# Eight experts of the first block: float32 weights, four experts on quarters of the columns

## The chip, the core and the metric

One core of one Trainium2 chip runs the whole program. The metric is the device time of one launch in microseconds (us). The kernel before takes 1819.28 us, the median of three runs that lie between 1818.02 and 1819.74. The engines are named as in the profile: PE is the matrix engine (TensorE), PEld its weight loads, DVE the VectorE, ACT the ScalarE, POOL the GpSimd, SP the engine that issues most transfers.

## What is computed

Four layers act on 256 tokens of 1024 features. Layers one and two (attention mixers, then a dense feed-forward and a layer of 8 experts) make the first block; layers three and four (two recurrent mixers, each with a layer of 16 experts) the second. The change is in the expert layer of the first block:

```python
def swiglu(h, w_gu, w_dn):
    gu = h @ w_gu
    g, u = jnp.split(gu, 2, axis=-1)
    return (jax.nn.silu(g) * u) @ w_dn

def moe_swiglu(h, w_router, w_gu_e, w_dn_e):     # 8 experts, w_gu 1024 x 2816, w_dn 1408 x 1024
    logits = (h @ w_router).astype(jnp.float32)
    top_val, top_idx = lax.top_k(logits, TOP_K)  # TOP_K = 2
    top_w = jax.nn.softmax(top_val, axis=-1)
    combine = jnp.sum(jax.nn.one_hot(top_idx, N_EXPERTS, dtype=jnp.float32) * top_w[..., None], axis=-2)
    ...
    for e in range(N_EXPERTS):
        out = out + combine[..., e:e + 1] * swiglu(h, w_gu_e[e], w_dn_e[e])
```

Each token goes to 2 of 8 experts, so an expert gets 64 of the 256 tokens on average; on the reference's inputs the fullest gets 76. All is float32.

## The kernel before

**Slots.** `moe1` works on gathered tokens. `router` and `ranks` give each chosen token a slot number within its expert, and a one-hot matrix `P` of 128 slots per expert gathers the tokens by a product (`gather`). An expert with more tokens than slots is done again by `overflow`, behind a branch on a count (`flag`); on these inputs it isn't entered.

**Split weights.** Everything that is multiplied with weights goes through a split of float32 numbers into a high and a low part of the faster type float32r: `hilo` (L462) lets ACT write the high part and DVE the difference. A product then is three matmuls (`mm3`): high by high, high by low, low by high. Weights arrive in tiles `raw` of 128 x 2048 float32 (a unit, 1 MB), five of them in a ring (`rp`), are split by `split` into tiles `hi` and `lo` (six each, `sp`), and the matmuls read these.

**The loop of the first expert layer.** `experts` runs jobs of (expert, 256 columns of gate and up): 8 chunks of the 1024 features give gate and up side by side in one bank of PSUM (512 columns), `swiglu` makes the hidden values, `turn` transposes them and splits them into `fh` and `fl`, and `down` adds their product with the matching rows of the second weight to two banks per expert. Six jobs to an expert, the last half as wide; the products up and down alternate. When an expert is finished its 128 x 1024 result is split (`y_split`), scattered back to the tokens by a product with the transposed one-hot matrix (`scatter`) and added to `xt` with the router's weight.

**Filling the router's wait.** The choice of experts is a chain of small DVE operations. While it runs, PE computes half of the first expert's first job for all 256 tokens (`dense` in `router`, whose weights are split ahead, partly into tiles `wide`), and only the hidden values are gathered later (`early`).

**The other expert layers** (`moe2`, `pairs`) already keep their weights float32: units go to a ring of 11 places (`RING`; five `raw`, six pairs of `hi` and `lo` tiles), are read by PE as they are, and two experts of 64 slots each stand on the two halves of the array's 128 columns: each matmul has a stationary operand 64 columns wide, and its result lands on half of the partitions. In these layers the router's wait is not filled. The program writes one float32 matmul; the trace shows two records for it.

**Order.** SP issues all weight transfers in the order that `sequence` lists, each as soon as its tile is free. The order on the engines is that of the code, except that a scheduler moves an instruction ahead where another would wait.

Of the kernel before, what the change touches and what calls it, by code (L numbers as in the profile page):

```python
# [9 lines left out]
F32 = mybir.dt.float32  # L10
F32R = mybir.dt.float32r
# [7 lines left out]
T = 256  # L19
# [10 lines left out]
HALF = 64  # L30
RING = 11
# [77 lines left out]

def rows_dn(w):  # L110
    return units(rows_k(w)[None])


def pack(inp):
# [29 lines left out]
    out["m1d"] = np.stack([rows_k(a["w_dn_exp"][0][e]) for e in range(NE1)])  # L144
# [42 lines left out]
class Kern:  # L187
# [123 lines left out]
    def sequence(self):  # L311
# [11 lines left out]
        m1 = []  # L323
        for e in range(NE1):
            for j in range(6):
                g = [(p["m1g"][e, 2 * j + i], UNIT) for i in range(2 if j < 5 else 1)]
                n = min((j + 1) * UNIT, FE * 8)
                m1.append((g, [(p["m1d"][e, :, j * UNIT:n], n - j * UNIT)]))

# [7 lines left out]
        jobs(m1)  # L337
# [24 lines left out]
    def load_plain(self):  # L362
# [12 lines left out]
        for h in range(2):  # L375
            for o in range(0, UNIT // 2, m):
                s = h * UNIT // 2 + o
                self.nc.sync.dma_start(halves[h][:, o:o + m], ap[:, s:s + m])
# [763 lines left out]

    def gather_spare(self, hh, hl):
# [296 lines left out]

    def overflow(self, flag, rk, C, hh, hl, n, F, gu, dn, after=None, cap=CAP):
# [7 lines left out]
        with tc.If(v > cap):  # L1449
# [9 lines left out]
            with tc.For_i(0, n, 1) as e:  # L1459
# [3 lines left out]
                for j in range(nt):  # L1463
# [16 lines left out]
                    nc.sync.dma_start(wt[:, :nch].rearrange("p k n -> p (k n)"), dn(e, j, nch * D))  # L1480
# [21 lines left out]
    def moe1(self):  # L1502
        nc = self.nc
        h = [self.xn[tb] for tb in range(2)]
        ps, hh, hl = self.router("router1", h, NE1)
# [8 lines left out]
        for tb in range(2):  # L1514
            self.dense(tb, range(0 if tb else EARLY, KC))
        first = self.gather(hh, hl, rk, 0)
# [12 lines left out]
        self.tt(C, C, o2, ALU.add)  # L1529
        m1g, m1d = self.p["m1g"], self.p["m1d"]  # L1530

        def add(b, tb, hf, n, ps):
            if b == NE1 - 1 and tb and hf:
                t = self.w2([128, 512], name="part")
                nc.scalar.activation(t, ps, AF.Copy, scale=C[:, tb, b:b + 1])
                nc.gpsimd.tensor_tensor(out=self.xt[:, tb, n], in0=self.xt[:, tb, n], in1=t, op=ALU.add)
            else:
                self.stt(self.xt[:, tb, n], ps, C[:, tb, b:b + 1], self.xt[:, tb, n], ALU.mult, ALU.add)
        jobs = [(e, 256 if j < 5 else 128, j == 0, j == 5, 0) for e in range(NE1) for j in range(6)]
        self.experts(jobs, hh, hl, rk, first, None, add)  # L1540
# [5 lines left out]
        def dn(e, j, n):  # L1546
# [506 lines left out]
```

## Time and profile before

| | us |
|---|---|
| median of three runs | 1819.28 |
| the profiled execution | 1816.75 |
| its span | 1815.0 |
| PE busy in it | 1755.0 (97%) |
| DVE busy, ACT busy | 1073.0, 849.3 |
| first expert layer, from the first gathering matmul to the last scattering one | 411.1 |

The page gives the span in 40 slices of 45.4 us. PE is at nine tenths or more nearly everywhere; the transfers run at 409 GB/s in the two later expert layers and at 320 to 360 GB/s in the first. A matmul's record is longer than the time it occupies the engine, since matmuls are pipelined: what one costs in a stream is the distance of two starts.

### The profile page before, as it was taken

Reading aid. Unit: us, or ns where it says so; the run is one execution under the profiler, and the core shown is the slowest. Engines: PE = TensorE matmul, PEld = TensorE weight load, DVE = VectorE, ACT = ScalarE, POOL = GpSimd, SP = SyncE. Lnnn points to the kernel's source line nnn. Section 1 sums busy time; section 2 is a strip of 40 time slices with the busy share of each in tenths; the row PEclk is TensorE's granted clock in tenths of the full one; section 3 lists DMA queues with packets and bytes.
Section 4 is the critical chain, followed back from the end, with each engine's and each line's share of the span. In section 5 each row is a group of like instructions: output and inputs, shape, how many; then the busy total and the mean of one; then the engine's idle time right before and its main releaser. Section 6 shows DMA issues by size and latency. Waiting matters only on the chain. (4 is left out here: it accounts for less than half of the span.)

```text
span 1815.0 us, 24991 instructions
## 1 busy us (share of the span) xinstructions
PE 1755.0 (97%) x9506; PEld 1279.4 (70%) x9506; DVE 1073.0 (59%) x1616; ACT 849.3 (47%) x1255; POOL 40.3 (2%) x59
## 2 busy tenths in 40 slices
PE   9999999999999999999999899899988998999996
PEld 7977899989878888888887787533424997443332
DVE  6567655455677999998989667321215687222123
ACT  5675544455855777777767542210103654111011
POOL 0000000000000000000000001000000001000000
PEclk9999999999999999999999999899998999999999
DMA  8445555546446599999999745699999556799996
GB/s 333 147 150 180 176 185 185 185 148 200 143 154 226 188 333 325 363 320 335 329 334 332 253 147 181 254 409 409 409 409 343 192 175 220 279 409 409 409 409 240
DMA packets 136436, 491.35 MB, mean 271 GB/s; under 512 B 15329, under 2 KB 15585, under 8 KB 136306
## 3 DMA queue, kind: packets, MB, share of 16 engines
q1 hardware_dynamic: 133794, 480.72, 73.0%
q0 software_dynamic: 2512, 8.91, 1.5%
q8 instruction: 79, 1.29, 0.3%
q14 instruction: 51, 0.42, 0.1%
HBM read 488.52 MB, written 1.05 MB: 270 GB/s over the span
## 5 line engine op out<-in xcount | busy, mean ns | idle before, releaser
L305 DVE TENSOR_TENSOR lo<-raw,hi 128x1024 fp32r<-128x1024 f32 x513 | 616.5, 1220 | 211.6 <-ACT hi L463 200.0
L463 ACT CAST hi<-raw 128x1024 fp32r<-128x1024 f32 x513 | 530.4, 1049 | 247.3 <-PE mm L274 167.1
L274 PE MATMUL mm<-hi,Th 128*128 128x512 f32 (+1 forms) x940 | 364.4, 388 | 2.2 <-ACT Th L463 1.9
L274 PE MATMUL mm<-lo,Th 128*128 128x512 f32 (+1 forms) x940 | 356.5, 379 | 0.6 <-DVE lo L305 0.5
L274 PE MATMUL mm<-hi,Tl 128*128 128x512 f32 (+1 forms) x940 | 356.4, 379 | 0.3 <-DVE Tl L305 0.3
L274 PE MATMUL mm<-Th,hi 128*128 128x256 f32 x768 | 218.0, 284 | 0.0
L274 PE MATMUL mm<-Th,lo 128*128 128x256 f32 x768 | 217.3, 283 | 0.0
L274 PE MATMUL mm<-Tl,hi 128*128 128x256 f32 x768 | 217.2, 283 | 0.0
L274 PEld LDWEIGHTS mm<-hi,Th 128*128 128x128 f32 x940 | 178.8, 190 | 36.3 <-ACT Th L463 4.1
L274 PEld LDWEIGHTS mm<-hi,Tl 128*128 128x128 f32 x940 | 178.1, 190 | 35.9 <-DVE Tl L305 3.3
L274 PEld LDWEIGHTS mm<-lo,Th 128*128 128x128 f32 x940 | 178.8, 190 | 32.6 <-DVE lo L305 2.3
L308 DVE SCALAR_TENSOR_TENSOR hh<-sl,gt,mm 128x256 f32<-128x256 f32 x33 | 15.9, 480 | 243.3 <-ACT sl L445 243.2
L445 ACT ACTIVATE sl<-mm 128x256 f32<-128x256 f32 (+2 forms) x93 | 36.9, 396 | 248.8 <-PE mm L274 248.3
L274 PEld LDWEIGHTS mm<-Th,hi 128*128 128x128 f32 x768 | 147.2, 192 | 1.5 <-ACT hi L463 0.8
L274 PEld LDWEIGHTS mm<-Tl,hi 128*128 128x128 f32 x768 | 147.2, 192 | 0.5
L274 PE MATMUL mm<-raw,xs 128*64 128x512 f32 x512 | 146.9, 598 | 0.6 <-DMA raw<-in_m 0.6
L274 PEld LDWEIGHTS mm<-Th,lo 128*128 128x128 f32 x768 | 147.2, 192 | 0.1
L274 PE MATMUL mm<-hi,xs 128*64 128x512 f32 x272 | 99.5, 603 | 9.0 <-DMA hi<-in_m 8.9
L274 PE MATMUL acc<-hi,fl 128*128 128x512 f32 x264 | 103.9, 397 | 0.6 <-DVE fl L305 0.6
L274 PE MATMUL acc<-lo,fh 128*128 128x512 f32 x264 | 104.4, 395 | 0.0
L274 PE MATMUL acc<-hi,fh 128*128 128x512 f32 x264 | 103.7, 396 | 0.4 <-ACT fh L463 0.4
L274 PE MATMUL mm<-lo,xs 128*64 128x512 f32 x272 | 94.0, 592 | 0.0
(397 smaller groups left out, 2023.2 us busy)
## 6 DMA issues: line engine op xcount, KB each, us to landing
raw<-in_wd SPq DMA_DIRECT2D x250, 512.0 KB, 4.9
raw<-in_m SPq DMA_DIRECT2D x184, 512.0 KB, 10.2
raw<-in_m1g SPq DMA_DIRECT2D x176, 512.0 KB, 6.0
lo<-in_m SPq DMA_DIRECT2D x104, 512.0 KB, 10.2
hi<-in_m SPq DMA_DIRECT2D x104, 512.0 KB, 10.2
raw<-in_m1d SPq DMA_DIRECT2D x87, 512.0 KB, 6.0
bg<-in_b_gate POOLq DMA_DIRECT2D x8, 256.0 KB, 3.6
bc<-in_ln_g POOLq DMA_DIRECT2D x4, 512.0 KB, 6.8
```

The costliest lines, as they stand in the source:

```text
L274: q = self.nc.tensor.matmul(out, lhsT, rhs, start=start, stop=stop, skip_group_check=True)
L305: return self.nc.vector.tensor_tensor(out=out, in0=in0, in1=in1, op=op)
L308: return self.nc.vector.scalar_tensor_tensor(out, in0, scalar, in1, op0=op0, op1=op1)
L445: q = self.nc.scalar.activation(*a, **k)
L463: a = self.nc.scalar.copy(hi, src)
```

## The change

The first expert layer leaves the split of its weights. Its units go to the ring of 11, PE reads them as float32, and four experts at a time stand on the four quarters (32 columns) of the array. An expert has 96 slots now, in three rounds of 32: for every chunk of weights each of the three rounds runs four matmuls, one to an expert (`products`). All of the products up of four experts come first (six steps over the columns), then the products down in two passes, one for each half of the 1024 output columns, over 11 chunks of hidden values. The second weight is laid out anew for that (`rows_h`). `gather12` gathers the slots of four experts in float32, 8 times four matmuls of 384 columns. The router's weight goes into the hidden values (`gate`), so that `add` only adds. `turn` and `scatter` are put off to the middle of the next step (`put_off`). `router` is called with `plain`: the dense half job is gone, and so is what it needed. `overflow` gets the new limit of 96 and the new layout.

```diff
@@ -28,6 +28,8 @@
 FE2 = 512
 CAP = 128
 HALF = 64
+QUART = 32
+ROUNDS = 3
 RING = 11
 ALPHA = (2 * DEPTH) ** 0.25
 RMS_EPS = 1e-6
@@ -105,6 +107,12 @@
 def half_cols(w, i):
 
     return w.rearrange("p (a n) -> p a n", a=2)[:, :, i * 128:(i + 1) * 128]
+
+
+def rows_h(w):
+
+    K, N = w.shape
+    return w.reshape(K // 128, 128, 2, N // 2).transpose(1, 2, 0, 3).reshape(128, -1)
 
 
 def rows_dn(w):
@@ -141,7 +149,7 @@
     out["wd"] = np.concatenate(dense, 0)
     gu = a["w_gu_exp"][0]
     out["m1g"] = np.stack([tiles_gu(gu[e][:, :FE], gu[e][:, FE:]) for e in range(NE1)])
-    out["m1d"] = np.stack([rows_k(a["w_dn_exp"][0][e]) for e in range(NE1)])
+    out["m1d"] = np.stack([rows_h(a["w_dn_exp"][0][e]) for e in range(NE1)])
     out["m2"] = np.stack([
         np.concatenate([tiles_gu(a["moe_w1_2"][l][e], a["moe_w3_2"][l][e]), rows_dn(a["moe_w2_2"][l][e])], 0)
         for l in range(DEPTH) for e in range(NE2)])
@@ -320,13 +328,6 @@
                 seq.append((wd[u], UNIT))
                 u += 1
         dense(2 * nd["mix"] + nd["ffn"])
-        m1 = []
-        for e in range(NE1):
-            for j in range(6):
-                g = [(p["m1g"][e, 2 * j + i], UNIT) for i in range(2 if j < 5 else 1)]
-                n = min((j + 1) * UNIT, FE * 8)
-                m1.append((g, [(p["m1d"][e, :, j * UNIT:n], n - j * UNIT)]))
-
         def jobs(js):
             for i, (g, d) in enumerate(js):
                 seq.extend(g)
@@ -334,7 +335,17 @@
                     seq.extend(js[i - 1][1])
             seq.extend(js[-1][1])
             seq[-1] += (True,)
-        jobs(m1)
+
+        n, nf = len(seq), FE * 4
+        for e0 in range(0, NE1, 4):
+            es = range(e0, e0 + 4)
+            seq.extend((p["m1g"][e, i], UNIT) for i in range(11) for e in es)
+            for hf in range(2):
+                for o in range(0, nf, UNIT):
+                    w = min(UNIT, nf - o)
+                    seq.extend((p["m1d"][e, :, hf * nf + o:hf * nf + o + w], w) for e in es)
+        seq[-1] += (True,)
+        self.plain.update((n + i, i % RING) for i in range(len(seq) - n))
         for l, nm in enumerate(("gla", "mlstm")):
             dense(nd[nm])
             m2 = lambda e, u: (p["m2"][l * NE2 + e, u], UNIT)
...
@@ -1138,6 +1151,25 @@
                     self.mm(v[:, dd], x[tb][:, c], P[:, tb].rearrange("p i s -> p (i s)"),
                             start=dd == 0 and i == 0, stop=dd == 1 and i == 3)
             (nc.vector.tensor_copy if d % 4 else nc.scalar.copy)(xs[:, d:d + 2], v)
+        return xs, P
+
+    def gather12(self, hh, hl, rk, e0):
+
+        nc = self.nc
+        n = ROUNDS * 128
+        shape = [128, ROUNDS, 4, QUART]
+        P = [self.w2([128, n], F32R, name="P") for _ in range(2)]
+        for tb in range(2):
+            q = self.tt(P[tb].rearrange("p (r x s) -> p r x s", r=ROUNDS, x=4),
+                        self.bf["iota"][:, :ROUNDS * QUART].rearrange("p (r s) -> p r s", r=ROUNDS)[:, :, None, :]
+                        .to_broadcast(shape), rk[:, tb, None, e0:e0 + 4, None].to_broadcast(shape), ALU.is_equal)
+        self.fence = q
+        xs = [self.tp.tile([128, 4, n], F32, name="xs", tag="Th") for _ in range(2)]
+        for d in range(KC):
+            ps = self.bank()[:, :n]
+            for i, (x, tb) in enumerate((x, tb) for x in (hh, hl) for tb in range(2)):
+                self.mm(ps, x[tb][:, d * 128:(d + 1) * 128], P[tb], start=i == 0, stop=i == 3)
+            (nc.vector.tensor_copy if d % 2 else nc.scalar.copy)(xs[d // 4][:, d % 4], ps)
         return xs, P
 
     def gather_spare(self, hh, hl):
@@ -1437,6 +1469,111 @@
         p, yh, yl = down(*last, ahead=True)
         self.scatter(yh, yl, PT[p // 2][:, p % 2], final, pre)
         return res
+
+    def fours(self, hh, hl, rk, first, Cs, add):
+
+
+        nc = self.nc
+        X, PT, gate, f, late = {}, {}, {}, {}, []
+        quarters = [slice(x * QUART, (x + 1) * QUART) for x in range(4)]
+
+        def more(g, P):
+            blocks = []
+            for r0 in range(0, ROUNDS, 2):
+                m = min(2, ROUNDS - r0)
+                v = self.bank()[:, :m * T].rearrange("p (e t) -> p e t", e=m)
+                for r in range(m):
+                    for tb in range(2):
+                        self.mm(v[:, r, tb * 128:(tb + 1) * 128], P[tb][:, (r0 + r) * 128:(r0 + r + 1) * 128],
+                                self.identr, start=r == 0 and tb == 0, stop=r == m - 1 and tb == 1)
+                t = self.w2([128, m, T], F32R, name="PT")
+                nc.scalar.copy(t, v)
+                blocks += [t[:, r] for r in range(m)]
+            PT[g] = blocks
+            pg = self.bank("acc")[:, :8 * ROUNDS]
+            for r in range(ROUNDS):
+                for tb in range(2):
+                    self.mm(pg[:, 8 * r:8 * r + 8], P[tb][:, r * 128:(r + 1) * 128], Cs[:, tb, g],
+                            start=r == 0 and tb == 0, stop=r == ROUNDS - 1 and tb == 1)
+            gt = gate[g] = self.wp.tile([128, 4], F32, name="gt", tag="gt", bufs=4)
+            v = pg.rearrange("p (r i n) -> p r n i", r=ROUNDS, i=2)
+            for x, s in enumerate(quarters):
+                nc.vector.tensor_reduce(gt[s, :ROUNDS], v[s, :, x], AX.X, ALU.add)
+
+        def gather(g):
+            X[g], P = self.gather12(hh, hl, rk, 4 * g) if g else first
+            if g:
+                more(g, P)
+
+        def products(out, w, lhs, k, rhs, start, stop):
+            for r in range(ROUNDS):
+                for x, s in enumerate(quarters):
+                    c = r * 128 + x * QUART
+                    self.mm(out[r][s, :w], lhs[:, c:c + QUART], rhs[x](k)[:, :w], start=start, stop=stop)
+
+        def turn(g, j, w, h, tag):
+            if j == 0:
+                t = [self.tp.tile([128, 5, ROUNDS * 128], F32, name="f", tag="Tl") for _ in range(2)]
+                for c in range(10):
+                    f[c] = t[c // 5][:, c % 5]
+            for kk in range(w // 128):
+                c = 2 * j + kk
+                if c == 10:
+                    f[c] = self.w2([128, ROUNDS * 128], name="f10")
+                ps = self.bank(tag)[:, :ROUNDS * 128]
+                for r in range(ROUNDS):
+                    nc.tensor.transpose(ps[:, r * 128:(r + 1) * 128], h[r][:, kk * 128:(kk + 1) * 128], self.ident)
+                (nc.vector.tensor_copy if kk else nc.scalar.copy)(f[c], ps)
+
+        def scatter(g, hf, ys, tag):
+            n = slice(hf * 512, (hf + 1) * 512)
+            for tb in range(2):
+                ps = self.bank(tag)
+                s = slice(tb * 128, (tb + 1) * 128)
+                for r in range(ROUNDS):
+                    self.mm(ps, PT[g][r][:, s], ys[r][:, 0], start=r == 0)
+                    self.mm(ps, PT[g][r][:, s], ys[r][:, 1], stop=r == ROUNDS - 1)
+                add(tb, n, ps)
+
+        def put_off():
+            while late:
+                late.pop(0)()
+
+        gather(0)
+        for g in range(NE1 // 4):
+            for j in range(6):
+                w, kpu = (256, 4) if j < 5 else (128, 8)
+                out = [self.bank("acc" if j % 2 else "mm") for _ in range(ROUNDS)]
+                for k in range(KC):
+                    if k % kpu == 0:
+                        ws = [self.unit(kpu) for _ in range(4)]
+                    if k == 4:
+                        put_off()
+                    products(out, 2 * w, X[g][k // 4][:, k % 4], k % kpu, ws, k == 0, k == 7)
+                if g == 0 and j == 0:
+                    more(0, first[1])
+                h = [self.w1([128, 256], name="hh") for _ in range(ROUNDS)]
+                for r in range(ROUNDS):
+                    self.swiglu(h[r][:, :w], out[r][:, :w], out[r][:, w:2 * w], gate[g][:, r:r + 1])
+                late.append(lambda g=g, j=j, w=w, h=h: turn(g, j, w, h, "acc" if j % 2 else "mm"))
+            for hf in range(2):
+                tag = "acc" if hf else "mm"
+                out = [self.bank(tag) for _ in range(ROUNDS)]
+                for c in range(11):
+                    if c % 4 == 0:
+                        ws = [self.unit(4) for _ in range(4)]
+                        if g and hf and c == 8:
+                            self.split()
+                    if c == 4:
+                        put_off()
+                        if hf and g + 1 < NE1 // 4:
+                            gather(g + 1)
+                    products(out, 512, f[c], c % 4, ws, c == 0, c == 10)
+                ys = [self.a4([128, 2, 512], F32R, name="ys") for _ in range(ROUNDS)]
+                for r in range(ROUNDS):
+                    self.hilo(ys[r][:, 0], ys[r][:, 1], out[r])
+                late.append(lambda g=g, hf=hf, ys=ys, tag=tag: scatter(g, hf, ys, tag))
+        put_off()
...
@@ -1511,9 +1649,7 @@
         S = self.rt(NE1, "S", BF)
         self.tt(S, o1, o2, ALU.add)
         rk, flag = self.ranks(S, NE1, "r")
-        for tb in range(2):
-            self.dense(tb, range(0 if tb else EARLY, KC))
-        first = self.gather(hh, hl, rk, 0)
+        first = self.gather12(hh, hl, rk, 0)
         e = self.rt(1, "gm")
         self.tt(e, m2, m1, ALU.subtract)
         self.act(e, e, AF.Exp)
@@ -1527,25 +1663,24 @@
         self.tt(C, o1, g1.to_broadcast([128, 2, NE1]), ALU.mult)
         self.tt(o2, o2, g2.to_broadcast([128, 2, NE1]), ALU.mult)
         self.tt(C, C, o2, ALU.add)
+        Cs = self.wp.tile([128, 2, 2, 8], F32R, name="Gs", tag="Gs", bufs=1)
+        self.hilo(Cs[:, :, :, :4], Cs[:, :, :, 4:], C.rearrange("p b (g j) -> p b g j", g=2))
         m1g, m1d = self.p["m1g"], self.p["m1d"]
 
-        def add(b, tb, hf, n, ps):
-            if b == NE1 - 1 and tb and hf:
-                t = self.w2([128, 512], name="part")
-                nc.scalar.activation(t, ps, AF.Copy, scale=C[:, tb, b:b + 1])
-                nc.gpsimd.tensor_tensor(out=self.xt[:, tb, n], in0=self.xt[:, tb, n], in1=t, op=ALU.add)
-            else:
-                self.stt(self.xt[:, tb, n], ps, C[:, tb, b:b + 1], self.xt[:, tb, n], ALU.mult, ALU.add)
-        jobs = [(e, 256 if j < 5 else 128, j == 0, j == 5, 0) for e in range(NE1) for j in range(6)]
-        self.experts(jobs, hh, hl, rk, first, None, add)
+        def add(tb, n, ps):
+            self.tt(self.xt[:, tb, n], self.xt[:, tb, n], ps, ALU.add)
+        self.fours(hh, hl, rk, first, Cs, add)
         self.prefetch()
...
```

On PE, between the router's last products and the first gathering, before (`Th`, `Tl` are the tokens' parts, `wide` and `hi`, `lo` the first expert's weights):

```order
L274 MATMUL acc<-Th,router_249 16x128 x8
L274 MATMUL acc<-Tl,router_249 16x128 x8
L274 MATMUL acc<-router1s,lt 128x8
L274 MATMUL acc<-hi,Th 128x256
L274 MATMUL acc<-lo,Th 128x256
L274 MATMUL acc<-hi,Tl 128x256
L274 MATMUL acc<-wide,Th 128x256
L274 MATMUL acc<-router1s,lt 128x8
L274 MATMUL acc<-wide,Th 128x256
L274 MATMUL acc<-wide,Tl 128x256
```

and after:

```order
L282 MATMUL acc<-Th,router_249 16x128 x8
L282 MATMUL acc<-Tl,router_249 16x128 x8
L282 MATMUL acc<-router1s,lt 128x8 x2
L282 LDWEIGHTS stri_b
L282 MATMUL mm<-S,stri_b 128x8
L282 LDWEIGHTS stri_b
L282 MATMUL mm<-S,stri_b 128x8
L282 LDWEIGHTS ones_b
L282 MATMUL mm<-S,ones_b 128x8
```

The 48 dense matmuls between the router, the count of ranks (`S` by `stri_b` and `ones_b`) and the gathering are gone, and nothing stands in their place.

On PE, in the middle of the layer, before (end of a job's products up, then its neighbour's products down):

```order
L274 MATMUL mm<-hi,Th 128x512
L274 MATMUL mm<-lo,Th 128x512
L274 MATMUL mm<-hi,Tl 128x512
L274 MATMUL acc<-hi,fh_7804 128x512
L274 MATMUL acc<-lo,fh_7804 128x512
L274 MATMUL acc<-hi,fl_7805 128x512
```

and after (from one step's transposes to the next step's; a step is 8 chunks by 12 matmuls, so 96):

```order
L1525 MATMUL mm<-ident,hh 128x128 x6
L282 MATMUL acc<-raw,xs 32x512 x48
L282 MATMUL mm<-hi,xs 32x512 x24
L282 MATMUL mm<-lo,xs 32x512 x24
L1525 MATMUL acc<-ident,hh 128x128 x6
```

Three matmuls over the whole array became float32 matmuls on 32 columns each, and the full-width work (transposes, scattering) stands as blocks between them.

On SP, where the layer's weights begin, before:

```order
L359 DMA raw<-in_wd 128x1024 x170
L359 DMA raw<-in_m1g 128x1024 x6
L359 DMA raw<-in_m1d 128x1024 x2
L359 DMA raw<-in_m1g 128x1024 x3
L359 DMA raw<-in_m1d 128x1024 x2
L359 DMA raw<-in_m1g 128x1024 x5
L1446 TENSOR_LOAD flag
```

and after:

```order
L370 DMA raw<-in_wd 128x1024 x170
L391 DMA raw<-in_m1g 128x1024 x10
L391 DMA hi<-in_m1g 128x1024
L391 DMA lo<-in_m1g 128x1024
L391 DMA hi<-in_m1g 128x1024
L391 DMA lo<-in_m1g 128x1024 x2
```

The loads into `hi` and `lo` tiles are new: 11 units instead of 5 can lie ready, and no ACT or DVE stands between a load and PE.

## Rows read from the trace of the kernel before

**Rows 1.** Stretches: busy us of PE, PEld, DVE, ACT, POOL; clock, DMA share, GB/s

```profile
599.70:1010.80 411.10, 408.90 (x1981) 336.94 (x1979) 380.56 (x436) 308.88 (x394) 0.00 (x0) 1.00 0.91 324
1200.00:1250.00 50.00, 49.92 (x220) 20.55 (x220) 13.65 (x27) 6.55 (x14) 0.42 (x1) 1.00 1.03 409
```

**Rows 2.** Groups of PE's instructions by form, 599.69 to 1010.8: count, busy us, mean ns

```profile
L274 PE MATMUL mm<-hi,Th 128*128 128x512 f32 x312 | 125.2, 401 | 0.3 <-ACT hi L463 0.3
...
L274 PE MATMUL acc<-lo,fh 128*128 128x512 f32 x176 | 69.6, 395 | 0.0
...
L274 PE MATMUL mm<-hi,Th 128*128 128x256 f32 x68 | 19.8, 291 | 0.0
...
L274 PE MATMUL mm<-yh,PT 128*128 128x512 f32 x32 | 12.5, 402 | 0.4 <-ACT yh L463 0.4
```

**Rows 3.** PE in order of time, the first expert layer: start us, duration us

```profile
1002.29 0.28 PE L274 MATMUL mm<-lo,Th 128*128 128x256 f32 x1
1002.41 0.28 PE L274 MATMUL mm<-hi,Tl 128*128 128x256 f32 x1
...
1004.76 0.39 PE L274 MATMUL acc<-lo,fh 128*128 128x512 f32 x1
1004.99 0.40 PE L274 MATMUL acc<-hi,fl 128*128 128x512 f32 x1
```

**Rows 4.** PE in order of time, the second block's experts, two on halves

```profile
1161.66 0.64 PE L274 MATMUL mm<-raw,xs 128*64 128x512 f32 x1
1161.67 0.64 PE L274 MATMUL mm<-hi,xs 128*64 128x512 f32 x1
1162.14 0.59 PE L274 MATMUL mm<-raw,xs 128*64 128x512 f32 x1
...
1162.57 0.59 PE L274 MATMUL mm<-raw,xs 128*64 128x512 f32 x1
...
1164.71 0.59 PE L274 MATMUL mm<-raw,xs 128*64 128x512 f32 x1
1165.24 0.44 PE L1374 MATMUL mm<-ident,hh 128*128 128x128 f32 x2
1165.61 0.65 PE L274 MATMUL mm<-hi,xs 128*64 128x512 f32 x2
```

**Rows 5.** PE in order of time: two float32 matmuls over all columns, four records

```profile
1381.11 1.98 PE L274 MATMUL mm<-xt,ident 128*128 128x512 f32 x4
```

**Rows 6.** DMA issues of the layer's weights: count, KB each, us to landing

```profile
raw<-in_m1g SPq DMA_DIRECT2D x176, 512.0 KB, 6.0
...
raw<-in_m1d SPq DMA_DIRECT2D x87, 512.0 KB, 6.0
```

**Rows 7.** PE in order of time, from the count of ranks to the gathering

```profile
597.80 0.20 PE L274 MATMUL mm<-S,stri_b 128*128 128x8 bf16 x2
...
599.69 0.65 PE L274 MATMUL mm<-P,hnh 128*128 128x256 f32 x4
```

**Rows 8.** The same place of the second block, where nothing fills the wait

```profile
1145.88 0.22 PE L274 MATMUL mm<-S,stri_b 128*128 128x16 bf16 x2 [4.98 <-DVE S L305]
...
1147.02 0.98 PE L274 MATMUL mm<-P,hnh 128*128 128x256 f32 x3 [0.83 <-DVE flag L1097]
...
1153.66 7.09 PE L274 MATMUL mm<-raw,xs 128*64 128x512 f32 x32
```

**Rows 9.** The clock in that place, as rows 1

```profile
1145.00:1150.00 5.00, 3.28 (x19) 3.22 (x20) 2.48 (x18) 0.80 (x2) 0.00 (x0) 0.50 0.00 0
```

**Rows 10.** PE in order of time at the layer's end, then DVE

```profile
1007.35 0.63 PE L274 MATMUL acc<-hi,fl 128*128 128x512 f32 x2
...
1009.71 1.09 PE L274 MATMUL mm<-yl,PT 128*128 128x512 f32 x4
1014.46 0.87 PE L477 MATMUL mm<-ident,xt 128*128 128x128 f32 x3 [3.66 <-PEq L1449]
...
1008.40 1.29 DVE L305 TENSOR_TENSOR yl<-acc,yh 128x512 fp32r<-128x512 f32 x2
```

More of the change, by code (lines that the diff above doesn't have):

```diff
@@ L377, in load_plain @@
                 s = h * UNIT // 2 + o
-                self.nc.sync.dma_start(halves[h][:, o:o + m], ap[:, s:s + m])
+                w = min(m, n - s)
+                if w > 0:
+                    self.nc.sync.dma_start(halves[h][:, o:o + w], ap[:, s:s + w])
         self.raws.append((halves, n, m))
@@ L1479, in overflow @@
                     wt = self.tp.tile([128, 2, D], F32, name="wd", tag="Tl")
-                    nc.sync.dma_start(wt[:, :nch].rearrange("p k n -> p (k n)"), dn(e, j, nch * D))
+                    for to, ap in dn(e, j, nch, wt):
+                        nc.sync.dma_start(to, ap)
                     for kk in range(nch):
@@ L1504, in moe1 @@
         h = [self.xn[tb] for tb in range(2)]
-        ps, hh, hl = self.router("router1", h, NE1)
+        ps, hh, hl = self.router("router1", h, NE1, True)
         self.tables("natural_log_exp_and_others")
@@ L1544, in gu, with dn @@
             return m1g[bass.ds(e, 1), u].rearrange("a p n -> (a p) n")
-        def dn(e, j, n):
-            return m1d[bass.ds(e, 1), :, j * UNIT:j * UNIT + n].rearrange("a p n -> (a p) n")
-        self.overflow(flag, rk, C, hh, hl, NE1, FE, gu, dn)
+        def dn(e, j, nch, wt):
+            for hf in range(2):
+                o = hf * FE * 4 + j * 1024
+                yield (wt[:, :nch, hf * 512:(hf + 1) * 512],
+                       m1d[bass.ds(e, 1), :, o:o + nch * 512].rearrange("a p (k n) -> (a p) k n", k=nch))
+        self.overflow(flag, rk, C, hh, hl, NE1, FE, gu, dn, cap=ROUNDS * QUART)
     def stats(self, tb, i, t, n=2):
@@ L1990, in moe2, with dn @@
         self.prefetch()
-        def dn(e, j, n):
-            return m2l[bass.ds(e, 1), 4 + j, :, :n].rearrange("a p n -> (a p) n")
+        def dn(e, j, nch, wt):
+            yield (wt[:, :nch].rearrange("p k n -> p (k n)"),
+                   m2l[bass.ds(e, 1), 4 + j, :, :nch * D].rearrange("a p n -> (a p) n"))
         def again():
```

## Prediction

> **What bounds the kernel now.** I read the slices first, then the stretch from the first gathering matmul of the first expert layer to its last scattering one. There PE is busy 408.9 of 411.1 us at full clock; DVE is busy 381 and ACT 309 us, both with splitting, and the transfers run at 324 GB/s [rows 1]. So PE ends last, with DVE close behind, and a change that only spares DVE and ACT gives nothing. That PE really streams shows in its groups and in the order of time: three groups of 312 matmuls and three of 176, all of 512 columns, and three of 68 of 256 columns [rows 2]; two of 512 columns start 0.23 us apart (0.233 over several), two of 256 columns 0.12 us [rows 3]. 1464 x 0.233 = 341.1, 204 x 0.12 = 24.5, 128 gathering matmuls x 0.12 = 15.4, 64 scattering ones [rows 2] x 0.233 = 14.9: together 395.9 us. 15 us are left for transposes, the one-hot transposes and gaps; some 5 us of these I count as gaps.
>
> **What a float32 matmul costs.** The second block shows it. A float32 matmul leaves two records. With two experts on halves of the columns both halves start within 0.01 us of each other, and the next pair of records 0.43 us later (1162.14 to 1162.57) [rows 4]; so two matmuls of 512 columns together take 2 x 0.428 = 0.856 us. A float32 matmul over all 128 columns takes the same: four records in 1.98 us, the last 0.6 us being its length, so some 0.46 us each at most [rows 5]. The time goes by moving columns, and what stands side by side in the array comes free, at least for two.
>
> **The change part by part.**
>
> Products. Before, an expert needs 66 chunks of 512 columns (8 x 5.5 up, 11 x 2 down) three times: 198 matmuls of 0.233 us. After, four experts need 66 chunks x 3 rounds, each a set of four matmuls. If the four quarters run side by side as the halves do, a set costs 0.856 us, and an expert 198 / 4 x 0.856 = 42.4 us against 46.1. In all: 372 sets of 512 columns x 0.856 = 318.4, and 48 sets of 256 columns (the last step) x 0.44 = 21.1; 339.5 us against about 365 (341.1 + 24.5). No row shows four quarters. The set costs 0.856 us if they all run together and 1.712 us if only two do. I take 0.856, since both rows with one and two side by side give it, and 0.876 as the upper end of that case: 32 records of pairs from 1153.66 to the next other work at 1160.67 make 0.438 each [rows 8]. That would add 8 us.
>
> Other work of PE. Two transposes between pairs take 0.47 us with both changes of shape (from 1164.71 + 0.43 to 1165.61) [rows 4]; 10 blocks of six transposes and two of three make 10 x 0.95 + 2 x 0.6 = 10.7. Gathering: 2 x 32 matmuls of 384 columns, between 0.12 and 0.233 [rows 3], 0.177 x 64 = 11.3. One-hot transposes and gates: 24 x 0.12 = 2.9. Scattering: 48 x 0.233 = 11.2. Six more changes of shape at 0.23 = 1.4. Together 37.5, and 377.0 with the products.
>
> The router's wait. The 48 dense matmuls between router and gathering go. They covered the chain of small DVE operations; nothing covers it now. Nine of them stood inside the chain, which moves the count of ranks up by 9 x 0.12 = 1.1 us, from 597.80 [rows 7] to 596.7. In the second block the gathering follows that count by 1.14 us (1145.88 to 1147.02) [rows 8]; so it begins at 597.8 instead of 599.69. But PE has then idled some 3 to 4 us. In the second block it idled 5 us at that place, the granted clock was 0.50 afterwards (the lower of its two levels, 1.2 of 2.4 GHz) [rows 9], and 32 gathering matmuls took 6.64 us (1147.02 to 1153.66) [rows 8] instead of 32 x 0.12 = 3.84. I charge the same 2.8 us; the bounds are nothing and, for 384 columns, all of 32 x 0.177 = 5.7.
>
> End of the layer. The results are split once more and scattered; DVE needs 0.65 us for each of three rounds (1.29 for two) [rows 10], so the last scattering waits some 1.6 us. The branch behind it holds PE 3.66 us before as after [rows 10]. The next layer's weights find only one tile free before the end, four after it; the second block's expert layers hand over the same way. I charge 0.5 us for this and for the first copy before the products.
>
> Splitting. 176 + 88 transfers' worth of tiles [rows 6] are no longer split: DVE and ACT lose most of their 381 and 309 us here. That is worth nothing by itself, as PE was full.
>
> Transfers. 264 transfers of 512 KB [rows 6] are 138 MB, 11 units (11.5 MB) of which lie ready at the start. The first places come free after the first half step, about 597.8 + 9 + 10.3 = 617. At the 409 GB/s of the second block [rows 1] the other 127 MB take 310 us, until 927; PE needs until about 975. A half step wants 4 units, 4.2 MB: 10.25 us at that rate, against 12 x 0.856 = 10.27 on PE. So the ring stays ahead, with little room.
>
> Sum: 377.0 + 2.8 + 1.6 + 0.5, and 3 us of gaps (before had some 5): 385 us from 597.8, so 982.8 instead of 1010.8, a gain of 28 us. The slots suffice (76 of 96), so the branch stays shut. The profiled execution would go from 1816.75 (span 1815.0) to 1788.7; it lies 0.14% under the median, which would go to 1791. With the bounds above, not all at one end, the likeliest case reaches from 1780 to 1804.
>
> **The rivals.**
>
> *Two quarters at a time (slower).* A pass reads 128 x 512 float32 for each matmul. Before, PE never reads faster than two such streams in 0.428 us [rows 4], about the same as one in 0.233 [rows 3]; four in 0.428 would be twice what any row shows. If that is the limit of reading, a set costs 1.712, and 396 sets (the 48 half ones counted as 24) another 339 us: 2130. The change loses from the point where a set costs more than 0.856 + 28 / 396 = 0.93 us, a stretch of 8%. Against it: that halves show no loss at all against one matmul.
>
> *The quarters cost something (slower).* They overlap, but not wholly; halfway between the two ends a set takes 1.28 us: 396 x 0.428 = 169 more, 1960. For it, as above, that no row shows four streams. The Trainium skill (TensorE: Matmul & The Clock Gate, Measured speedup vs the span model) gives 2.38 times for three column tiles, which is 0.79 of full; by that rule a set would take 1.08 us and the kernel 1880, an estimate. No run here shows quarters, and the halves in the trace lose nothing.
>
> *The transfers end last.* At 324 GB/s their engines are already busy 0.91 [rows 1]. If they stay at that rate, 127 MB take 392 us from 617, until 1009, and half a step and the scattering follow (8 us): 1017, 6 us later than now: 1826. It decides below 127 MB / 358 us = 354 GB/s. Against it: transfers of the same size run at 409 where PE lets them.
>
> *Equal.* Loads of the stationary operand, waits or changes of shape eat 25 us: the set at 0.92, or each change of shape a microsecond dearer. About 1816; it is part of the slight stretch below.
>
> **How the numbers follow.** Forecast (1780 to 1804) 0.69; below it 0.02; a slight stretch of the set (1804 to 1828) 0.09; transfers last (1815 to 1828) 0.05; quarters that cost 0.07; two at a time 0.08. The measurement tells about 0.2% (3.6 us) from no change. Faster: 0.69 + 0.02 + 0.05 of the slight stretch = 0.76; same: 0.02 + 0.02 = 0.04; slower: 0.20. The range leaves out the last two rivals and what lies below: 1780 to 1828 holds 0.83.
>
> **What would show it.** In the profile after: records of the quarters' matmuls in fours, starting together, the next four 0.428 us on; PE full from about 605 to 980 at full clock, DVE and ACT nearly idle there; transfers near 360 GB/s with pauses. The clock falls once after the router. A next four at 0.5 us or more, or records two by two, shows the rivals of the array; PE waiting for `raw`, `hi` or `lo` from DMA at 1.0 DMA share shows the transfers. I am wrong if the last scattering stands later than 1007, or if the time goes outside the layer.

## The result and the profile after

The changed kernel takes 1797.07 us, the median of four runs (1796.89 to 1797.69), beside 1818.65 for the kernel before, measured with it: a ratio of 0.9883, 95% interval 0.9866 to 0.9900. It is faster by 21.6 us. The forecast was 1791, a gain of 28; the range (1780 to 1828) holds the time. The profiled execution has a span of 1795.3 us instead of 1815.0.

The stretch from the first gathering matmul of the changed layer to the end of its last scattering one shows the work as foretold. The columns are those of [rows 1]:

```profile
core 0: us, PE busy (x) PEld busy (x) DVE busy (x) ACT busy (x) POOL busy (x), PEclk, DMA share, GB/s
599.06:990.33 391.27, 390.74 (x3562) 145.60 (x3562) 44.95 (x89) 34.96 (x76) 0.00 (x0) 0.99 0.88 332
```

DVE falls from 381 to 45 us, ACT from 309 to 35, and PE is as full as before. The layer takes 391.3 us instead of 411.1; 385 were forecast.

The four quarters run side by side. PE in order of time (start, duration; `raw` and `hi` are the tiles in which the weights of the four experts lie):

```profile
617.70 0.59 PE L282 MATMUL mm<-raw,xs 128*32 128x512 f32 x1
617.71 0.60 PE L282 MATMUL mm<-hi,xs 128*32 128x512 f32 x3
618.13 0.59 PE L282 MATMUL mm<-raw,xs 128*32 128x512 f32 x1
618.14 0.61 PE L282 MATMUL mm<-hi,xs 128*32 128x512 f32 x3
...
640.67 0.88 PE L1525 MATMUL mm<-ident,hh 128*128 128x128 f32 x6
...
662.22 0.87 PE L1525 MATMUL acc<-ident,hh 128*128 128x128 f32 x6
```

Four records start within 0.01 us, the next four 0.43 us later, just as the pairs of [rows 4] do. From one block of transposes to the next, 24 sets and the block, it takes 21.55 us; the forecast's terms make 24 x 0.856 + 0.95 = 21.49.

What doesn't fit comes later in the layer, most of it with the second group of four experts. There a block of transposes comes nine matmuls after a step's end, instead of 48:

```profile
864.66 0.59 PE L282 MATMUL acc<-raw,xs 128*32 128x512 f32 x1
864.66 0.60 PE L282 MATMUL acc<-hi,xs 128*32 128x512 f32 x2
...
866.80 0.59 PE L282 MATMUL acc<-raw,xs 128*32 128x512 f32 x1
866.81 0.60 PE L282 MATMUL acc<-hi,xs 128*32 128x512 f32 x2
867.34 0.87 PE L1525 MATMUL mm<-ident,hh 128*128 128x128 f32 x6
868.14 1.47 PE L282 MATMUL acc<-hi,xs 128*32 128x512 f32 x3
869.03 0.62 PE L282 MATMUL acc<-raw,xs 128*32 128x512 f32 x1
```

Ahead of the block three records start together, six times from 864.66 on: three matmuls each of three quarters (a matmul leaves two records), and none of the fourth. The order of the matmuls in the program says the same. With A to D for the quarters it reads, in the changed kernel at this place:

```order
ABCABCABC, six transposes, DDDABCDABCD...
```

The scheduler has moved the fourth quarter's three matmuls behind the others', with the block in between. The order of the code is ABCDABCDABCD throughout. Behind the block the fourth quarter's records at 868.14 follow each other, three in 1.47 us, and it runs alone for 0.9 us until the others join at 869.03. The engine counts as busy all the while, so no table of waits shows this. A set whose four matmuls have been taken apart like this is called a cut set below.

Behind the layer comes the branch to the overflow code that isn't entered, and then the next layer. Columns as above, in brackets the idle time before and what ended it; "issue" means that the profile shows nothing that was waited for:

```profile
987.27 3.06 PE L282 MATMUL acc<-ys,PT 128*128 128x512 f32 x12
993.42 1.94 PE L490 MATMUL mm<-ident,xt 128*128 128x128 f32 x8 [3.09 <-PEq L1586]
...
999.31 0.59 PE L282 MATMUL mm<-hi,Th 128*128 128x512 f32 x1 [1.84 <-issue]
...
1003.10 0.71 PE L490 MATMUL mm<-ident,xt 128*128 128x128 f32 x5
```

The branch holds PE for 3.09 us, before 3.66 [rows 10]. But from the restart to the five transposes at 1003.10 it takes 9.68 us; before, the same stretch ran from 1014.46 [rows 10] to 1021.37, 6.91 us, without a stop in it:

```profile
1021.37 0.71 PE L477 MATMUL mm<-ident,xt 128*128 128x128 f32 x5
```

So the layer gave 6.3 us less than forecast, it began 1.3 us later than forecast (599.06, not 597.8), and the next layer's start cost 2.8 us more; the branch gave back 0.6. That is 9.7 us, of which 1.4 come back in later layers: a span 8.3 us over the forecast's 1787.0. The experiments ask what the 6.3 and the 2.8 are.

### The profile page after: what moved, and what is told of

The parts are those of the page before. It is cut to its first block, busy times and chain, and to the rows that moved or that the text cites. A ratio compares the mean times of both kernels' runs of the same rounds, so it can differ in the third digit from the quotient of the medians.

```text
span 1795.3 us, 26892 instructions
## 1 busy us (share of the span) xinstructions
PE 1731.1 (96%) x11041; PEld 1081.2 (60%) x11041; DVE 731.5 (41%) x1260; ACT 565.6 (32%) x927; POOL 39.1 (2%) x58
## 5 line engine op out<-in xcount | busy, mean ns | idle before, releaser
L313 DVE TENSOR_TENSOR lo<-raw,hi 128x1024 fp32r<-128x1024 f32 x250 | 304.3, 1222 | 209.2 <-ACT hi L476 192.3
L476 ACT CAST hi<-raw 128x1024 fp32r<-128x1024 f32 x250 | 260.5, 1049 | 227.3 <-PE mm L282 146.3
L282 PE MATMUL mm<-raw,xs 128*32 128x512 f32 (+1 forms) x1064 | 234.3, 595 | 0.5 <-DMA raw<-in_m 0.5
L282 PE MATMUL mm<-hi,Th 128*128 128x512 f32 (+1 forms) x560 | 219.4, 392 | 3.7 <-ACT Th L476 1.9
L282 PE MATMUL mm<-hi,Tl 128*128 128x512 f32 (+1 forms) x560 | 214.8, 384 | 0.3 <-DVE Tl L313 0.3
L282 PE MATMUL mm<-lo,Th 128*128 128x512 f32 (+1 forms) x560 | 214.5, 383 | 0.2 <-DVE lo L313 0.2
L282 PE MATMUL mm<-hi,xs 128*32 128x512 f32 (+1 forms) x572 | 149.2, 598 | 8.9 <-DMA hi<-in_m 8.8
L282 PE MATMUL mm<-lo,xs 128*32 128x512 f32 (+1 forms) x572 | 143.6, 592 | 0.0
L282 PE MATMUL acc<-raw,f 128*32 128x512 f32 (+1 forms) x484 | 118.2, 594 | 1.2 <-DMA raw<-in_m 1.2
L282 PE MATMUL acc<-raw,xs 128*32 128x512 f32 (+1 forms) x456 | 85.6, 548 | 0.0
```

The costliest lines, as they stand in the source:

```text
L282: q = self.nc.tensor.matmul(out, lhsT, rhs, start=start, stop=stop, skip_group_check=True)
L313: return self.nc.vector.tensor_tensor(out=out, in0=in0, in1=in1, op=op)
L476: a = self.nc.scalar.copy(hi, src)
```

## Experiments

| run | median us (lowest to highest) | ratio to before, 95% |
|---|---|---|
| changed kernel | 1797.07 (1796.89 to 1797.69) | 0.9866 to 0.9900 |
| e1 whole sets | 1786.18 (1784.29 to 1788.16) | 0.9808 to 0.9835 |
| e2 whole sets, blocks early | 1786.84 (1785.17 to 1787.47) | 0.9811 to 0.9838 |
| e3 quarters in a row | 1943.53, one run | |
| e4 two rounds (leaves tokens out) | 1746.88, one run | |
| e5 e1 and ring shift | 1784.25 (1784.08 to 1787.48) | 0.9801 to 0.9828 |
| e6 e1 and first wait filled | 1786.26 (1785.78 to 1791.83) | 0.9807 to 0.9834 |
| e7 e1 and all waits filled | 1784.17 (1783.46 to 1785.70) | 0.9795 to 0.9822 |
| e8 e1, ring shift, all waits filled | 1782.63 (1782.30 to 1783.13) | 0.9788 to 0.9815 |
| e9 changed kernel and 13 tiny matmuls | 1799.53 (1798.47 to 1800.87) | 0.9880 to 0.9910 |
| e10 changed kernel and 16 tiny matmuls | 1793.10 (1792.73 to 1794.02) | 0.9845 to 0.9875 |
| e11 e6 and 4 tiny matmuls | 1784.29 (1782.30 to 1784.52) | 0.9795 to 0.9822 |
| e12 e8 and 4 tiny matmuls | 1778.56 (1775.24 to 1779.17) | 0.9760 to 0.9786 |

### Cut sets: e1 and e2

Each matmul and transpose of the layer is tied behind the one that the code has before it, so that the scheduler can neither move a block into a set nor change the order of the quarters:

```diff
...
+    def chained(self, q):
+        if self.pin is not None:
+            if self.pin is not True:
+                self.order(q, self.pin)
+            self.pin = q
+        return q
...
```

> TensorE keeps the order of the code in the new layer, so that no set of four quarter-matmuls is cut by another block, and the transposes and scatterings stand 12 sets behind the step that feeds them. In the changed kernel six blocks (the one-hot transposes, three of the first group's and the second group's scatterings and three turns) stand inside a set. Theory of cut sets: a part of a set takes as long as a whole one, 0.86 us, so six cuts cost 5.1 us, and the three early turns wait 0.5 us each for the hidden values: 6.6 us less, 1790.5 us, the distance from the first gathering matmul to the end of the last scattering one 385 instead of 391.3. Rival, the sets themselves are slower than 0.856 us or wait for weights: no change, 1797.

e2 moves the blocks forward without cutting a set:

```diff
-                    if k == 4:
+                    if k == 1:
                         put_off()
...
-                    if c == 4:
+                    if c == 1:
                         put_off()
```

> As the kernel with whole sets, but every turn and scattering stands 3 sets (2.57 us) behind the step that feeds it instead of 12; no set is cut. Theory: the hidden values of the third round are ready about 3.1 us behind the step's last product, so each of the 11 turns waits some 0.5 us and the three scatterings in the middle as much or more: 7 to 8 us slower than with 12 sets, about 1797 to 1798. Rival, only the cuts cost anything: the same time as with 12 sets, 1790.5.

e1 took 10.9 us off the changed kernel, more than the 6.6 expected. The expectation counted nine matmuls as two sets and one matmul; the order above shows that they are three matmuls each of three quarters. In the profiled executions 9.9 us of the gain lie in the layer, and 2.8 at the start of the next one, where the stop is down to 0.26 us; 1.8 are lost again at the branch (4.87 us instead of 3.09), and 1.8 in the rest of the program. The layer's stretch, then the same five blocks of the second group of experts (853.53, 867.34, 889.78, 911.38 and 933.78 in the changed kernel):

```profile
599.25:980.58 381.33, 380.51 (x3562) 139.80 (x3562) 44.95 (x89) 34.95 (x76) 0.00 (x0) 0.99 0.90 341
```

```profile
851.07 0.87 PE L1533 MATMUL acc<-ident,hh 128*128 128x128 f32 x6
872.61 0.87 PE L1533 MATMUL mm<-ident,hh 128*128 128x128 f32 x6
894.15 0.87 PE L1533 MATMUL acc<-ident,hh 128*128 128x128 f32 x6
910.57 0.87 PE L1533 MATMUL mm<-ident,hh 128*128 128x128 f32 x6
927.00 0.55 PE L1533 MATMUL acc<-ident,hh 128*128 128x128 f32 x3
```

The same 3562 records take 381.3 instead of 391.3 us. From the first to the last of these blocks it is 75.93 us against 80.25, so three cut turns (blocks of transposes) and one short wait (0.53 us) cost 4.3: some 1.3 us a cut, more than the 0.86 of a set. The two scatterings of the first group cost 2.9 (from the last turn at 738.59 to the next gathering at 770.43 it is 31.84 us, in the changed kernel 34.74), and the end of the second group 3.0. The layer's last products ahead of the last scattering, first in the changed kernel, then in e1:

```profile
984.61 2.74 PE L282 MATMUL acc<-raw,f 128*32 128x512 f32 x12
987.27 3.06 PE L282 MATMUL acc<-ys,PT 128*128 128x512 f32 x12
```

```profile
975.70 1.47 PE L283 MATMUL acc<-raw,f 128*32 128x512 f32 x12
977.10 3.48 PE L283 MATMUL acc<-ys,PT 128*128 128x512 f32 x12
```

Twelve records take 1.47 us where four quarters end together and 2.74 us where one has been left behind. Which part of the 2.9 and 3.0 is a cut and which a scattering that came close behind its split isn't told apart. Nor is it told apart what a block inside a set costs and what a quarter that is held back: e1 undoes both.

e2 measured the same as e1 (1786.84), where 1797 was expected: that theory fell, the rival holds. A block 3 sets behind its step doesn't wait. The estimate of 3.1 us had been read at 911.38, where the block stands behind nine matmuls of half width, three on each of three quarters, about 1.3 us after its step. So it is the cuts, not the nearness, that cost.

### Where the array's and the transfers' limits lie: e3 and e4

```diff
-            for r in range(ROUNDS):
-                for x, s in enumerate(quarters):
+            for x, s in enumerate(quarters):
+                for r in range(ROUNDS):
```

> As the kernel with whole sets, but for each chunk the three rounds of one quarter come one behind the other, then the next quarter. The same matmuls, the same operands. Theory, TensorE starts matmuls in the order of the program, and a quarter that is busy holds all that stand behind: for a chunk 9 steps of 0.856 us with one step shared with the next chunk, 8 instead of 3; 132 chunks x 5 x 0.856 = 565 us more, about 2356. Rival, each quarter runs ahead by itself: no change, 1791.

157 us more than e1: neither 565 nor none. One quarter of e3 in order of time:

```profile
642.94 0.59 PE L283 MATMUL acc<-raw,xs 128*32 128x512 f32 x1
...
643.37 0.59 PE L283 MATMUL acc<-raw,xs 128*32 128x512 f32 x1
...
643.80 0.59 PE L283 MATMUL acc<-raw,xs 128*32 128x512 f32 x1
...
645.18 0.62 PE L283 MATMUL acc<-raw,xs 128*32 128x512 f32 x1
...
645.63 0.59 PE L283 MATMUL acc<-raw,xs 128*32 128x512 f32 x1
```

The quarter works off its records 0.43 us apart and then stands still for 0.95 us. So a busy quarter holds up matmuls of other quarters that stand behind it, but not all of them; how far one may lag isn't settled. Of the orders tried here, only the four quarters in turn give the full rate.

```diff
-ROUNDS = 3
+ROUNDS = 2
...
-        self.overflow(flag, rk, C, hh, hl, NE1, FE, gu, dn, cap=ROUNDS * QUART)
+        self.overflow(flag, rk, C, hh, hl, NE1, FE, gu, dn, cap=96)
```

> Two rounds instead of three: the tokens beyond 64 of an expert are left out, so a third of the products and of the gathering, turning and scattering falls away; all weights are still read. TensorE then needs some 255 us for the layer, until 855, and the transfers end last. Theory of the sum: they run at the 409 GB/s of the second block, 127 MB from about 612 on take 310 us, until 922, and the last products and scatterings follow: the layer ends at 925 to 932, 58 to 65 us less, about 1735. Rival, the transfers have no more than the 333 GB/s that the stretch of the changed kernel shows: 381 us, until 993, no change, 1797.

Three stretches of 25 us:

```profile
650.00:675.00 25.00, 23.11 (x176) 6.73 (x180) 1.39 (x3) 1.14 (x3) 0.00 (x0) 1.00 1.03 409
800.00:825.00 25.00, 22.48 (x169) 6.45 (x172) 1.38 (x3) 1.14 (x3) 0.00 (x0) 1.00 1.02 408
900.00:925.00 25.00, 23.46 (x148) 8.68 (x149) 2.76 (x4) 1.17 (x2) 0.00 (x0) 1.00 1.02 402
```

With less work for PE the transfers run at the 409 GB/s of the second block [rows 1], and PE now waits for them (15 us in all for tiles that a transfer fills). The layer's last scattering ended at 939, 7 to 14 us later than expected, and the time is 1746.9 where 1735 was expected. The 332 GB/s of the changed kernel are what PE lets them have. With three rounds and whole sets the layer (381 us) stands some 40 us above that of e4 (340), where the transfers set the pace.

### The start of the layer: e6 and e7

```diff
+        self.busy(10, hh)
         rk, flag = self.ranks(S, NE1, "r")
+        self.busy(3, hh)
         first = self.gather12(hh, hl, rk, 0)
...
```

`busy` issues matmuls of 512 columns with `identr` into a bank that nobody reads.

> The kernel with whole sets, and TensorE runs 10 matmuls of 512 columns whose result nobody reads between the first router and the count of ranks, and 3 more before the gathering. Theory, the idle wait lowers the granted clock and the first gathering pays for it (about 7.9 us against 5.6 for the second group's): the gathering at 0.175 us a matmul, 2.3 us less, 1784. Rival, the clock falls anyway or the gathering waits for its operands: no change, 1786.

> As the kernel that fills the first router's wait, and in the two layers of the second block 20 such matmuls before the count of ranks and 3 before the gathering. There 32 gathering matmuls of 256 columns take 6.6 us behind a wait of 5 us, against 3.8 at full clock. Theory of the clock: 2.8 us less in each, 7.9 us less than with whole sets, 1778. Rival: 1784 or 1786, the filling matmuls give nothing there.

The clock (the column before the DMA share), first in the changed kernel, then in e6:

```profile
594.00:598.00 4.00, 1.44 (x18) 1.07 (x15) 2.78 (x20) 0.74 (x2) 0.00 (x0) 0.86 0.94 380
598.00:602.00 4.00, 3.05 (x14) 3.00 (x11) 1.85 (x10) 1.22 (x3) 0.00 (x0) 0.50 0.03 13
602.00:606.00 4.00, 4.00 (x20) 4.00 (x20) 1.46 (x3) 1.17 (x3) 0.00 (x0) 0.79 0.00 0
```

```profile
594.00:598.00 4.00, 3.94 (x26) 2.92 (x25) 2.84 (x20) 0.89 (x2) 0.00 (x0) 1.00 0.90 362
598.00:602.00 4.00, 3.85 (x21) 3.40 (x21) 2.31 (x10) 1.77 (x4) 0.00 (x0) 1.00 0.03 11
602.00:606.00 4.00, 4.00 (x32) 2.86 (x34) 1.64 (x3) 0.96 (x2) 0.00 (x0) 1.00 0.00 0
```

In e6 it stays at 2.4 GHz, and the gathering takes 5.76 us (598.90 to 604.66) instead of 7.89 in the changed kernel (599.06 to 606.95) and 8.38 in e1. The mechanism is right, but the time was 1786.26, no gain on e1; in e7 it was 2.0 us instead of the expected 7.9. The gain is lost again behind the branch, in a stop of 6.46 us in e6 and 4.24 us in e7 (and in the second of the two later layers e7's gathering gained 1.6 us, not 2.8). e1's line stands first, then e6's:

```profile
989.75 0.79 PE L283 MATMUL mm<-hi,Th 128*128 128x512 f32 x1 [0.26 <-issue]
```

```profile
983.01 0.45 PE L505 MATMUL mm<-ident,xt 128*128 128x128 f32 x1 [5.42 <-PEq L1604]
989.92 1.76 PE L505 MATMUL mm<-ident,xt 128*128 128x128 f32 x7 [6.46 <-issue]
```

In e1 PE had stopped there before the 15th matmul behind the branch (0.26 us), in the changed kernel before the 15th too (1.84 us), in e6 before the 2nd. The fill had put 13 matmuls ahead of the branch, and 15 - 2 = 13. The trace of e6 is of its longest run, 1791.83; its median is 5.6 us lower, so the stop was probably shorter in its other four runs.

### The stop behind the branch: e5, and e8 to e12

e5 asks whether the next layer's weights are late:

```diff
-        self.plain.update((n + i, i % RING) for i in range(len(seq) - n))
+        self.plain.update((n + i, (i + 7) % RING) for i in range(len(seq) - n))
```

> The kernel with whole sets, and the ring of the first expert layer begins at place 7 instead of 0, so that the layer's last units lie in the hi and lo tiles and the five raw tiles come free for the next layer's weights about 10 us earlier. After the layer's last scattering TensorE there waits 4.87 us at the branch, and the next layer's first matmuls are slow. Theory, the hand-over hangs on late weights: 2 us less, 1784. Rival, the next layer's first weights lie ready anyway and the wait at the branch doesn't depend on them: no change, 1786. Second rival, the branch waits longer while transfers run (3.09 us in the changed kernel where they pause, 4.87 with whole sets, 6.98 with two rounds): up to 2 us more, 1788.

> Whole sets, shifted ring and all three waits filled. If the three act on separate places their gains add: 1776 where the shift gives 2 us, 1778 where it gives nothing, 1780 where it costs 2.

e5 ended at 1784.25, 1.9 us under e1, but the runs of the two overlap; in its trace PE waits 2.39 us at the branch instead of 4.87 and then stops for 0.75. It is unclear in size, and the shorter wait isn't the shift's doing alone: e8 and e12 shift the ring too, and PE waits 4.95 and 4.81 us there. Why the branch holds PE for 4.8 to 5.4 us in the other runs with whole sets, and for 2.8 to 3.1 in the changed kernel, e9 and e10, isn't shown. e8 stayed 3 to 7 us behind what was expected, with a stop of 2.90 us before the 2nd matmul. The next two test the stop alone, in the changed kernel, by 13 and by 16 matmuls of 8 columns in the first router's wait:

```diff
+        self.busy(16, hh, 8)
         rk, flag = self.ranks(S, NE1, "r")
```

> The changed kernel as it is, with 13 matmuls of 8 columns more in the first router's wait, whose result nobody reads; some 0.06 us each, in a wait of 2.5 us. In the changed kernel TensorE stops 1.84 us before its 15th matmul behind the branch, with its operands there; in the three kernels with 13 more matmuls ahead of the branch it stops before the 2nd one, 2.9 to 6.5 us. Theory, the instructions come in pieces, the branch leads into the middle of one, and 13 more instructions ahead move the end of the piece 13 matmuls nearer: the stop stands before the 2nd matmul and lasts 3 to 6 us, 1798 to 1801. Rival, the stop is a wait for weights or a matter of the filled waits: no change, 1797.

> The same with 16 of these matmuls instead of 13. Theory of pieces: the branch then leads to the beginning of the next piece, no stop within the next 100 matmuls, 1.8 us less than the changed kernel, 1795, and 3 to 6 us less than with 13. Rival: 1797, the same as with 13.

First e9, then e10:

```profile
992.74 0.45 PE L497 MATMUL mm<-ident,xt 128*128 128x128 f32 x1 [2.84 <-PEq L1593]
999.08 1.65 PE L497 MATMUL mm<-ident,xt 128*128 128x128 f32 x7 [5.89 <-issue]
```

```profile
992.67 1.94 PE L497 MATMUL mm<-ident,xt 128*128 128x128 f32 x8 [3.04 <-PEq L1593]
995.45 0.84 PE L497 MATMUL mm<-ident,xt 128*128 128x128 f32 x3
...
999.72 0.71 PE L497 MATMUL mm<-ident,xt 128*128 128x128 f32 x5
```

Three tiny matmuls more, and the kernel is 6.4 us faster (1799.53 to 1793.10): with 13 a stop of 5.89 us before the 2nd matmul, with 16 none, and from restart to the five transposes 7.05 us, about what the kernel before needs (6.91). So the 2.8 us of the changed kernel come from this stop: 1.84 us are the stop itself, and the rest goes to a granted clock that is still 0.50 from 1001 to 1003 us, where e10 has 1.00 from 999 to 1001. e9 came in as expected by the theory of pieces; e10 is 1.9 us faster than the expected 1795, and 0.7 of that lies ahead of the branch. In the changed kernel the transfers of kind "instruction" show one packet of 0.02 MB between 996 and 997 us, ahead of the stop's end at 999.31 (packets, MB, share of the DMA engines' time in that microsecond):

```profile
q8 instruction: 1, 0.02, 5.7%
```

The other traces with such a stop show one too. By the times of the packets in them (us):

| run | PE restarts | packet begins | stop ends | from packet to end |
|---|---|---|---|---|
| changed kernel | 993.42 | 996.87 | 999.31 | 2.44 |
| e1 | 985.45 | 987.15 | 989.75 | 2.60 |
| e2 | 984.90 | 987.23 | 989.75 | 2.52 |
| e3 | 1139.45 | 1142.59 | 1145.08 | 2.49 |
| e5 | 982.90 | 984.83 | 987.25 | 2.42 |
| e6 | 983.01 | 987.53 | 989.92 | 2.39 |
| e7 | 983.03 | 985.40 | 987.71 | 2.31 |
| e8 | 982.58 | 983.53 | 985.92 | 2.39 |
| e9 | 992.74 | 996.80 | 999.08 | 2.28 |

The stop ends 2.3 to 2.6 us after its packet began, wherever it stands, which fits that PE waits for these instructions; whose they are the profile doesn't say. In e10, e11 and e12 such a packet begins 3.6, 1.5 and 0.3 us after the restart, and PE doesn't stop.

The Trainium skill (Runtime: NRT & Kernel Launch, Instruction fetch mechanics) says that an engine gets its instructions in blocks of 16 KiB, the next one while the current one runs, and that a taken branch out of the blocks at hand stalls. The traces agree, with 0.02 MB in a packet. That the next block is late too where the branch leads near the end of one, by up to 6.46 us, fits all of these runs; it is more than that page says. The stop is 6.46 us in e6, 4.24 in e7 and 2.90 in e8, at the same place, as the packet begins 4.5, 2.4 and 1.0 us after the restart; what sets that isn't settled.

> The kernel with whole sets that fills the first router's wait, and 4 matmuls of 8 columns more there. Theory of pieces: the stop of 6.46 us before the 2nd matmul behind the branch goes, and what filling the wait gained in the layer (2.1 us) stays: 1783 to 1784, where whole sets alone gave 1786.2. Rival: 1786.3 as without the 4.

> Whole sets, shifted ring, all three waits filled, and 4 matmuls of 8 columns more in the first. Theory of pieces: the stop of 2.90 us goes, 1779 to 1780. Rival: 1782.6 as without the 4.

Both came in within 0.5 us of what the theory gave: 1784.29 (e6 1786.26) and 1778.56 (e8 1782.63), without a stop in either trace. PE behind the branch, first e11, then e12:

```profile
982.31 1.94 PE L505 MATMUL mm<-ident,xt 128*128 128x128 f32 x8 [4.93 <-PEq L1604]
```

```profile
981.60 1.94 PE L505 MATMUL mm<-ident,xt 128*128 128x128 f32 x8 [4.81 <-PEq L1604]
```

e12 beats both kernels: 0.9773 of the one before (0.9760 to 0.9786), 18.5 us under the changed one.

## Why the prediction was right, and where its size was off

**Products.** Right to the hundredth: a set costs 0.856 us, two quarters at a time and quarters that cost fell at once. By the Trainium skill (TensorE: Matmul & The Clock Gate, Measured speedup vs the span model) three column tiles gave 2.38 times; here four give four times in a long stream (from 641.48 to 662.22 in the changed kernel 96 matmuls, 0.215 us each, where one alone takes 0.856), and the measurement decides.

**The sum of the layer.** From the gathering to the last scattering 385 us were forecast; with whole sets it is 381.3, so the terms were some 4 us too high: the wait at the end is below 1 us instead of 1.6 (in e1 the last scattering starts 977.10, some 0.5 us behind the products, and takes 0.4 us longer than 3.06), and few gaps are left. The changed kernel took 391.3. The step that failed is "3 us of gaps": it took the gaps from the kernel before, where a block between two matmuls costs only itself. With quarters, the scheduler also took sets apart, holding one quarter back with a block in between; a cut turn costs some 1.3 us, and that term is 9.9 us in all, as e1 shows.

**The router's wait.** The charge for the clock was about right (2.8 us; e6's gathering is 2.1 us shorter than the changed kernel's and 2.6 shorter than e1's). Wrong was that the count of ranks comes 1.1 us earlier: it started at 597.81 as before. In the changed kernel PE waits for the halves that it transposes for the router, 0.46 us at 591.04 and 0.16 us at 591.86; that the 9 dense matmuls had stood in such waits is read from the trace and was not tried.

**End and hand-over.** The branch did hold PE about as long as before (3.09 us for 3.66); with whole sets it is longer (4.87), which the forecast didn't weigh. The term of 0.5 us for the hand-over was mis-sized: 2.8 us, and its cause was none that the forecast weighed; late weights play at most a small part (e5), the place of the code does it (e9, e10).

**Splitting and transfers.** DVE and ACT became idle and that was worth nothing by itself, as said; 409 GB/s are there when PE asks for them (e4), so the transfers didn't end last.

**Direction.** The gain rested on 198 matmuls of 0.233 us for an expert against 198 quarters of a set of 0.856, and that held. With whole sets (e1) the gain is 31.8 us, more than the forecast's 28.

## What to carry to other kernels

Where matmuls run side by side on parts of the array, look in the order of the instructions for sets that have been taken apart: a cut with a block in it cost some 1.3 us here, the engine looked busy meanwhile, and tying the order by hand gave 9.9 us in the layer. Price a scheduler's placement from that order, not from gaps of a kernel with another grain. And when an edit that should gain a few microseconds gains none, look behind the branches: a handful of instructions ahead of one can move a stop by 6 us.

## What the runs showed of the hardware that was not expected

- A stop of up to 6.46 us behind a branch depends on the number of instructions ahead of it: 13 matmuls more bring it to the 2nd matmul, 16 remove it. In nine traces it ends 2.3 to 2.6 us after a packet of instructions has begun.
- Quarters aren't independent streams: three matmuls in a row on one quarter slow all four down, by 157 us over the layer, and yet not to one quarter at a time.
- Filling the waits of the three routers with matmuls that nobody reads keeps the granted clock at 2.4 GHz; in the first of the two later layers 32 gathering matmuls then take 3.9 us (1119.99 to 1123.93 in e7) instead of 6.6, in the second 4.0 instead of 5.6.
